# Logits ahead of x, and two even groups of 64 rows, in a top-2 mixture-of-experts dispatch kernel

## The chip, the cores and the metric

The kernel runs on one core of a Trainium2 chip. The metric is device time in microseconds of one execution; it is given as the median of several runs. The work on a core is shared between the engines VectorE (DVE in the profile), ScalarE (ACT), GpSimd (POOL), TensorE (PE, unused here) and SyncE (SP), and 16 DMA engines that move data between HBM, the large memory, and SBUF, the on-chip memory of 128 partitions. SP and ACT issue the DMA transfers here; each has a queue of its own (q1 and q10 in the profile).

## The reference

For each of 16 x 1024 = 16,384 tokens there is a vector x of 512 numbers and 8 router logits. The logits become probabilities, the two largest are scaled to sum to one, and the output has two copies of x for each token, one times each of the two weights, the smaller weight first:

```python
probs = np.exp(router_logits - logits_max)
probs = probs / np.sum(probs, axis=-1, keepdims=True)
topk_indices = np.argsort(probs, axis=-1)[..., -k:]
topk_probs = np.take_along_axis(probs, topk_indices, axis=-1)
topk_probs = topk_probs / np.sum(topk_probs, axis=-1, keepdims=True)
x_expanded = x[:, :, np.newaxis, :].repeat(k, axis=2)
return (x_expanded * topk_probs[..., np.newaxis]).astype(np.float32)
```

All is 32-bit floating point. The input x has 33.5 MB, the logits 0.5 MB, the output 67.1 MB.

## The kernel before, in words

The tokens are the rows of a matrix. They are cut into two groups (`GROUPS`, line 49), of 128 x 65 and 128 x 63 rows. Within a group partition p holds 65 (or 63) consecutive rows, so that what one partition reads or writes in HBM is one contiguous stretch: 65 rows of x are 130 KB, 65 rows of output 260 KB.

**Weights.** `top2_weights` (line 14) finds the largest and the second largest of the 8 logits of all 128 rows of each partition by a tournament of maxima and minima on VectorE (lines 27 to 37), subtracts them (line 40), and gets both weights as sigmoids of the difference on ScalarE (lines 42 and 43, into `WA`). The logits come in two transfers (lines 116 and 117), one for each group, which SP issues behind the first 16 rows of x.

**Products.** A group's x is loaded into `xs` in pieces of `LOADS` rows (line 51, issued at line 112). The multiplications at line 128 walk through the group by `plan`: each takes n rows from `xs`, doubles them, multiplies by the weights, and writes 2n rows. The output of the first 16 rows and of rows 32 to 47 goes into `osp`, a buffer of 16 doubled rows; that of the other rows goes back into `xs`, over rows which were already used. Where, is said by `over` (line 98): row r's output starts at `xs` row 2r - G, with G the rows of the group, so that the last output row ends at the end of `xs` (for rows 16 to 31 it is called with G = 32, and the output starts at `xs` row 0). `LAST` (line 54) lists the steps from row 48 on.

**Order.** Every product is followed by its store (line 136), which SP issues, but for the one of the first two rows, which ACT issues. Each engine executes its own instructions in the order in which they are written; SP therefore issues the loads of a group, then its stores one by one, each when its product is done, then the loads of the second group. A tile framework adds the waits that the use of buffers calls for: a load into rows of `xs` waits for the stores that still read them, a product into `osp` for the stores that read `osp`. Transfers issued by SP pass through the DMA engines in the order of issue, as the trace shows them.

Of the kernel before, what the change touches and what calls it, by code (L numbers as in the profile page):

```python
# [1 line left out]

# [4 lines left out]

F32 = mybir.dt.float32
ALU = mybir.AluOpType
ACTF = mybir.ActivationFunctionType  # L10
P = 128


def top2_weights(nc, pool, logits, M, E):

    hi, lo, n = None, None, E  # L20
    while n > 1:
        n //= 2
        if hi is None:
            a, b = logits[:, :, 0:n], logits[:, :, n : 2 * n]
            nhi = pool.tile([P, M, n], F32, tag=f"hi{n}")
            nlo = b
            nc.vector.tensor_tensor(nhi, a, b, op=ALU.max)  # L27
            nc.vector.tensor_tensor(nlo, a, b, op=ALU.min)  # L28
        else:
            a, b = hi[:, :, 0:n], hi[:, :, n : 2 * n]  # L30
            nhi = pool.tile([P, M, n], F32, tag=f"hi{n}")
            nlo = pool.tile([P, M, n], F32, tag=f"lo{n}")
            tmp = pool.tile([P, M, n], F32, tag=f"tmp{n}")
            nc.vector.tensor_tensor(tmp, lo[:, :, 0:n], lo[:, :, n : 2 * n], op=ALU.max)  # L34
            nc.vector.tensor_tensor(nlo, a, b, op=ALU.min)  # L35
            nc.vector.tensor_tensor(nlo, nlo, tmp, op=ALU.max)  # L36
            nc.vector.tensor_tensor(nhi, a, b, op=ALU.max)  # L37
        hi, lo = nhi, nlo
    dlt = pool.tile([P, M], F32, tag="dlt")
    nc.vector.tensor_tensor(dlt, hi[:, :, 0], lo[:, :, 0], op=ALU.subtract)  # L40
    WA = pool.tile([P, M, 2], F32, tag="WA")
    nc.scalar.activation(WA[:, :, 0], dlt, ACTF.Sigmoid, scale=-1.0)  # L42
    nc.scalar.activation(WA[:, :, 1], dlt, ACTF.Sigmoid, scale=1.0)  # L43
    return WA

GROUPS = [65, 63]

LOADS = [[2, 2, 4, 8, 17, 32], [16, 16, 31]]


LAST = [[(48, 9), (57, 8)], [(48, 15)]]


@with_exitstack
def kernel(
    ctx: ExitStack,
    tc: tile.TileContext,  # L60
    x: bass.AP,
    router_logits: bass.AP,
    k: bass.AP,
    out: bass.AP,
):
    nc = tc.nc
    B, S, D = x.shape
    E = router_logits.shape[-1]
    N = B * S
    assert int(k) == 2 and E == 8 and N == P * sum(GROUPS)  # L70
    M = N // P

    L = 16
    x_v, o_v, rl_v = [], [], []
    t0 = 0
    for n in GROUPS:
        t1 = t0 + P * n
        x_v.append(
            x.rearrange("b s d -> (b s) d")[t0:t1].rearrange("(p m) d -> p m d", p=P)
        )  # L80
        o_v.append(
            out.rearrange("b s k d -> (b s) k d")[t0:t1].rearrange(
                "(p m) k d -> p m k d", p=P
            )
        )
        rl_v.append(
            router_logits.rearrange("b s e -> (b s) e")[t0:t1].rearrange(
                "(p m) e -> p m e", p=P
            )
        )  # L90
        t0 = t1

    wpool = ctx.enter_context(tc.tile_pool(name="wpool", bufs=1))
    logits = wpool.tile([P, M, E], F32)
    xs = wpool.tile([P, max(GROUPS), D], F32)
    osp = wpool.tile([P, L, 2, D], F32)

    def over(r, n, G):

        a = 2 * r - G
        return xs[:, a : a + 2 * n, :].rearrange("p (r k) d -> p r k d", k=2)

    h = L // 2
    e = 2
    m0 = 0
    for g, G in enumerate(GROUPS):
        r = 0  # L110
        for n in LOADS[g]:
            nc.sync.dma_start(xs[:, r : r + n, :], x_v[g][:, r : r + n, :])  # L112
            r += n
            if g == 0 and r == L:

                nc.sync.dma_start(logits[:, :G], rl_v[0])  # L116
                nc.sync.dma_start(logits[:, G:], rl_v[1])
                WA = top2_weights(nc, wpool, logits, M, E)
        assert r == G
        begin = [(0, e, osp[:, :e]), (e, L - e, osp[:, e:])] if g == 0 else [(0, L, osp)]  # L120
        plan = begin + [
            (L, L, over(L, L, 2 * L)),
            (2 * L, h, osp[:, :h]),
            (2 * L + h, h, osp[:, h:]),
        ]
        plan += [(r, n, over(r, n, G)) for r, n in LAST[g]]
        for r, n, og in plan:
            nc.vector.tensor_tensor(  # L128
                og,
                xs[:, r : r + n, :].unsqueeze(2).to_broadcast([P, n, 2, D]),  # L130
                WA[:, m0 + r : m0 + r + n, :].unsqueeze(3).to_broadcast([P, n, 2, D]),
                op=ALU.mult,
            )

            queue = nc.scalar if n == e else nc.sync
            queue.dma_start(o_v[g][:, r : r + n], og)  # L136
        m0 += G


# [1 line left out]
_INS = ['x', 'router_logits', 'k']  # L141
_OUTS = [((16, 1024, 2, 512), 'float32')]

_NUMBERS = {'k': 2}


# [26 lines left out]
```

## Time and profile before

| what | value |
|---|---|
| median of 6 runs | 240.64 us (240.24 to 241.29) |
| profiled execution, its own time | 240.24 us |
| its span in the profile | 238.5 us |
| VectorE busy | 142.0 us (60%) in 23 instructions |
| ScalarE busy | 1.8 us |
| DMA | 101.19 MB in 3312 packets, mean 424 GB/s |
| multiplications (line 128) | 12, 138.2 us in all |
| longest wait of VectorE | 31.3 us, for a load of x |

The page cuts the span into 40 slices of about 6 us and gives for each the busy share of an engine in tenths; its DMA row is the mean over the 16 DMA engines. A queue's share is the time that its packets took, as a part of 16 engines' span. A packet is here what one partition gets or gives in one transfer, and each transfer ends with small packets that raise a semaphore. The trace also holds each packet's start, length and duration, which is where single packet times below come from. In the timeline a row has its start, its duration (of several merged instructions, from the first to the last), the engine ("SPq" is an issue by SP's queue), the line, the operation, what is written from what, and in brackets the idle time before it with what ended it.

### The profile page before, as it was taken

The page shows a single profiled execution, that of the slowest core. Times are in us where ns is not written, and L with a number is a line of the kernel's source. Part 1 is how long each engine was busy: PE and PEld are TensorE (multiplying, and loading weights), DVE is VectorE, ACT ScalarE, POOL GpSimd, SP SyncE. Part 2 cuts the span into 40 slices and gives each one's busy share as a digit, 9 for nine tenths or more (in the row PEclk, how much of TensorE's full clock was granted, in tenths as well). Part 3 has the DMA queues.
Part 4 walks back from the last instruction along what each step waited for, and adds up shares of the span by engine and source line. Part 5 has one row for each costly group of instructions (what it writes and reads, how often), then busy time and mean ns, then how long its engine had stood idle before and what let it go on. Part 6 is the DMA issues. An engine that isn't in the chain of part 4 may idle for free.

```text
span 238.5 us, 116 instructions
## 1 busy us (share of the span) xinstructions
DVE 142.0 (60%) x23; ACT 1.8 (1%) x3; POOL 0.2 (0%) x4
## 2 busy tenths in 40 slices
DVE  0058999990299699900000699999106999990000
ACT  2000000000000000000000000000000000000000
POOL 0000000000000000000000000000000000000000
DMA  7999999999798999999999999999998989999995
GB/s 254 441 464 402 539 407 396 374 462 462 341 517 352 440 440 440 440 402 478 440 434 412 423 484 437 415 473 396 396 484 374 506 352 440 440 440 429 495 423 237
DMA packets 3312, 101.19 MB, mean 424 GB/s; under 512 B 368, under 2 KB 496, under 8 KB 880
## 3 DMA queue, kind: packets, MB, share of 16 engines
q1 hardware_dynamic: 3168, 100.14, 97.8%
q10 hardware_dynamic: 144, 1.05, 1.0%
HBM read 34.08 MB, written 67.11 MB: 424 GB/s over the span
## 4 chain that ended last, share of the span: by engine, by line
DMA 43%; DVE 41%; issue 5%; SPq 1%; ACT 0%; DVEq 0%
DVE xs L128 22%; DVE osp L128 17%; DMA xs<-in_x_dram 13%; DMA out_dram<-osp 13%; DMA out_dram<-xs 12%; DMA logits<-in_router_logits_dram 5%; SPq L112 1%; DVE nhi L27 0%; SPq L116 0%; DVE logits L28 0%; DVE nlo L36 0%; DVE nhi L37 0%; DVE nlo L35 0%; DVE tmp L34 0%; SPq L136 0%
## 5 line engine op out<-in xcount | busy, mean ns | idle before, releaser
L128 DVE TENSOR_TENSOR osp<-xs,WA 128x8192 f32<-128x8192 f32 (+3 forms) x7 | 69.1, 9908 | 55.5 <-DMA xs<-in_x_dram 31.3
L128 DVE TENSOR_TENSOR xs<-xs,WA 128x16384 f32<-128x16384 f32 (+3 forms) x5 | 69.1, 13811 | 2.2 <-DMA out_dram<-xs 2.0
L27 DVE TENSOR_TENSOR nhi<-logits 128x512 f32<-128x512 f32 x1 | 0.7, 692 | 14.6 <-DMA logits<-in_router_logits_dram 14.6
L42 ACT ACT_TABLE_LOAD x1 | 1.3, 1283 | 0.7 <-PEq L154 0.7
L28 DVE TENSOR_TENSOR logits<-logits 128x512 f32<-128x512 f32 x1 | 0.7, 693 | 0.0
L35 DVE TENSOR_TENSOR nlo<-nhi 128x256 f32<-128x256 f32 (+1 forms) x2 | 0.7, 352 | 0.0
L37 DVE TENSOR_TENSOR nhi<-nhi 128x256 f32<-128x256 f32 (+1 forms) x2 | 0.7, 351 | 0.0
L36 DVE TENSOR_TENSOR nlo<-nlo,tmp 128x256 f32<-128x256 f32 (+1 forms) x2 | 0.7, 350 | 0.0
L42 ACT ACTIVATE WA<-dlt 128x128 f32<-128x128 f32 x1 | 0.3, 314 | 16.6 <-DVE dlt L40 16.6
L34 DVE TENSOR_TENSOR tmp<-logits 128x256 f32<-128x256 f32 x1 | 0.4, 417 | 0.0
L40 DVE TENSOR_TENSOR dlt<-nhi,nlo 128x128 f32<-128x128 f32 x1 | 0.3, 291 | 0.0
L43 ACT ACTIVATE WA<-dlt 128x128 f32<-128x128 f32 x1 | 0.3, 298 | 0.0
L34 DVE TENSOR_TENSOR tmp<-nlo 128x128 f32<-128x128 f32 x1 | 0.3, 283 | 0.0
L154 POOL MEMSET const-bfloat16-1.0<- 128x1 bf16 x1 | 0.1, 101 | 0.0
L154 POOL MEMSET const-uint8-127<- 128x1 uint8 x1 | 0.1, 101 | 0.0
L154 POOL MEMSET const-float32-0.0<- 128x1 f32 x1 | 0.1, 98 | 0.2 <-issue 0.2
L154 POOL MEMSET const-float32-1.0<- 128x1 f32 x1 | 0.1, 98 | 0.0
## 6 DMA issues: line engine op xcount, KB each, us to landing
out_dram<-osp SPq DMA_DIRECT2D x4, 4096.0 KB, 20.7
xs<-in_x_dram SPq DMA_DIRECT2D x2, 4096.0 KB, 29.9
xs<-in_x_dram SPq DMA_DIRECT2D x1, 7936.0 KB, 37.9
out_dram<-xs SPq DMA_DIRECT2D x1, 7680.0 KB, 23.2
out_dram<-osp SPq DMA_DIRECT2D x1, 7168.0 KB, 27.5
out_dram<-xs SPq DMA_DIRECT2D x1, 4608.0 KB, 20.4
xs<-in_x_dram SPq DMA_DIRECT2D x1, 4352.0 KB, 21.0
out_dram<-xs SPq DMA_DIRECT2D x1, 4096.0 KB, 21.6
```

Of the source, the lines that this page charges most:

```text
L27: nc.vector.tensor_tensor(nhi, a, b, op=ALU.max)
L28: nc.vector.tensor_tensor(nlo, a, b, op=ALU.min)
L34: nc.vector.tensor_tensor(tmp, lo[:, :, 0:n], lo[:, :, n : 2 * n], op=ALU.max)
L35: nc.vector.tensor_tensor(nlo, a, b, op=ALU.min)
L36: nc.vector.tensor_tensor(nlo, nlo, tmp, op=ALU.max)
L37: nc.vector.tensor_tensor(nhi, a, b, op=ALU.max)
L40: nc.vector.tensor_tensor(dlt, hi[:, :, 0], lo[:, :, 0], op=ALU.subtract)
L42: nc.scalar.activation(WA[:, :, 0], dlt, ACTF.Sigmoid, scale=-1.0)
L43: nc.scalar.activation(WA[:, :, 1], dlt, ACTF.Sigmoid, scale=1.0)
L112: nc.sync.dma_start(xs[:, r : r + n, :], x_v[g][:, r : r + n, :])
L128: nc.vector.tensor_tensor(og, xs[:, r : r + n, :].unsqueeze(2).to_broadcast([P, n, 2, D]), WA[:, m0 + r : m0 + r + n, :].unsqueeze(3).to_b ...
L154: nc = _bacc.Bacc("TRN2", target_bir_lowering=False, num_devices=1)
```

## The change

The groups become even, 64 rows per partition each, with loads, steps and last steps to match (17 becomes 16, 9 becomes 8, 31 becomes 32, 15 becomes 16). One partition's stretch is then 128 KB of x and 256 KB of output in either group. The logits come in one transfer instead of two: for each partition, two parts of 2 KB, one for each group. It is issued by SP ahead of the loads of x, and `top2_weights` is called right behind it.

```diff
-GROUPS = [65, 63]
-LOADS = [[2, 2, 4, 8, 17, 32], [16, 16, 31]]
-LAST = [[(48, 9), (57, 8)], [(48, 15)]]
+GROUPS = [64, 64]
+LOADS = [[2, 2, 4, 8, 16, 32], [16, 16, 32]]
+LAST = [[(48, 8), (56, 8)], [(48, 16)]]
...
-        rl_v.append(
-            router_logits.rearrange("b s e -> (b s) e")[t0:t1].rearrange(
-                "(p m) e -> p m e", p=P
-            )
-        )
         t0 = t1
+    rl_v = router_logits.rearrange("b s e -> (b s e)").rearrange(
+        "(g p r) -> p g r", g=len(GROUPS), p=P
+    )
 
     wpool = ctx.enter_context(tc.tile_pool(name="wpool", bufs=1))
     logits = wpool.tile([P, M, E], F32)
+    nc.sync.dma_start(
+        logits.rearrange("p m e -> p (m e)").rearrange(
+            "p (g r) -> p g r", g=len(GROUPS)
+        ),
+        rl_v,
+    )
+    WA = top2_weights(nc, wpool, logits, M, E)
+
     xs = wpool.tile([P, max(GROUPS), D], F32)
     osp = wpool.tile([P, L, 2, D], F32)
...
             nc.sync.dma_start(xs[:, r : r + n, :], x_v[g][:, r : r + n, :])
             r += n
-            if g == 0 and r == L:
-
-                nc.sync.dma_start(logits[:, :G], rl_v[0])
-                nc.sync.dma_start(logits[:, G:], rl_v[1])
-                WA = top2_weights(nc, wpool, logits, M, E)
         assert r == G
```

More of the change, by code (lines that the diff above doesn't have):

```diff
@@ L73 @@
     L = 16
-    x_v, o_v, rl_v = [], [], []
+    x_v, o_v = [], []
     t0 = 0
```

## The prediction

> **What bounds the kernel now.** I began with the slices of the page and its table of queues.
>
> ```profile
> DVE  0058999990299699900000699999106999990000
> ACT  2000000000000000000000000000000000000000
> POOL 0000000000000000000000000000000000000000
> DMA  7999999999798999999999999999998989999995
> ...
> q1 hardware_dynamic: 3168, 100.14, 97.8%
> q10 hardware_dynamic: 144, 1.05, 1.0%
> HBM read 34.08 MB, written 67.11 MB: 424 GB/s over the span
> ```
>
> VectorE has long idle stretches; the DMA engines have none. The packets of both queues took 97.8% + 1.0% = 98.8% of 16 engines' span, 235.6 us out of 238.5. The packet records of the trace agree: the first packet starts at 1.73 us, the last ends at 237.25, and in these 235.5 us all the places where an engine stood empty add up to 0.48 us (mean of the 16 engines). So the span is 1.7 us before the first packet, 235.5 us of packets back to back, and 1.2 us behind the last; the profiled run's own time, 240.24 us, has 1.74 us more around the span, and the median of the runs is another 0.40 us above it.
>
> Next I asked the timeline for what orders the queue.
>
> ```profile
> 0.72 1.80 SPq L112 DMA_DIRECT2D xs<-in_x_dram  x4
> 2.57 0.69 SPq L116 DMA_DIRECT2D logits<-in_router_logits_dram  x1
> 3.30 0.47 SPq L117 DMA_DIRECT2D logits<-in_router_logits_dram  x1
> 3.81 1.06 SPq L112 DMA_DIRECT2D xs<-in_x_dram  x2
> 14.64 0.69 DVE L27 TENSOR_TENSOR nhi<-logits 128x512 f32<-128x512 f32 x1 [14.64 <-DMA logits<-in_router_logits_dram]
> ...
> 36.44 0.35 SPq L136 DMA_DIRECT2D out_dram<-osp  x1
> ...
> 83.32 18.48 DVE L128 TENSOR_TENSOR xs<-xs,WA 128x9216 f32<-128x9216 f32 x2 [2.04 <-DMA out_dram<-xs]
> ...
> 102.25 21.60 SPq L112 DMA_DIRECT2D xs<-in_x_dram  x3
> ...
> 198.24 16.16 DVE L128 TENSOR_TENSOR xs<-xs,WA 128x15360 f32<-128x15360 f32 x1
> 214.43 0.33 SPq L136 DMA_DIRECT2D out_dram<-xs  x1
> ```
>
> VectorE starts late, at 14.64 us, and still each SP transfer is issued before the engines have drained those ahead of it. The store issued at 36.44 has its first packet at 46.23, behind the x loads; the last store, issued at 214.43, has its first packet at 218.57, so it waited 4.1 us in the ring. That backlog is what to check: an edit to an engine's order is worth nothing while it stays, and costs what it lacks if it goes.
>
> **The change, part by part.** *Bytes and packets.* 65 + 63 rows become 64 + 64, so the 101.19 MB stay. Packets of data stay at 128 for each x load and store and 256 for the logits (2,080 and 2,016 B before, 85 and 82 ns each; 2,048 B after, 83.5 ns by their mean). There is one transfer fewer, so one 9 ns semaphore packet less on each engine. Sum: -0.01 us. A packet of 32,768 B takes 1,213 ns and one of 65,536 B takes 2,418, a fixed 8 ns and 27.2 GB/s for each engine; 17-, 9-, 15- and 31-row transfers becoming 16, 8, 16 and 32 rows shift 8 ns at most. Zero.
>
> *The logits go to the head of SP.* L116 (0.69 us) and L117 (0.47 us) leave their place, and one issue comes in front of the x loads. How long an issue with two parts per partition takes isn't in the trace: between one x issue (0.38 us, after which the first packet came 0.63 us later) and L116 plus L117 (1.16 us), so the first packet comes 0 to 0.8 us later than now. I take the L116 row, 0.69 us in place of 0.38, less what earlier landing work hides: +0.2 us. The x issues follow every 0.43 us, while the logits hold each engine for 16 x 83.5 ns = 1.34 us, so no hole opens behind them. The slow first reads (the 4,096 B packets took 197 ns in the mean against 159 usual: 16 per engine, 0.61 us) are paid by whichever packets are first.
>
> The logits now land at about 4.5 us (1.9 + 1.34 + 0.6 for the slow first reads + 0.4 to signal), in place of 14.6. L27 to L40 take 3.9 us and the two sigmoids 0.55, so the first product starts at about 9 rather than 19.12. The second needs 16 rows of x, which land 1.2 us later than now (0.52 MB at 434 GB/s are ahead): 13.2 + 1.2 = 14.4, then 15.1 us of VectorE, its store issued at 29.6 instead of 36.44. Ahead of it in the ring are 18.35 MB (x, logits, ACT's store of the first two rows), 42.3 us, so its first packet goes at about 45.5, against 46.23. Seven microseconds earlier on VectorE lie wholly behind the loads. If that cover were gone the gain would be up to 7 us, but bytes forbid it.
>
> *Even groups.* With G=64 the outputs of rows 48 on start at xs row 32; with 65 they start at 31, inside the region that the store of rows 16 to 32 still reads. So VectorE's 2.04 us wait at 83.3 goes, and the second load of group two no longer waits for a store from xs. Behind SP's waiting load stood only the next loads. Both waits lie under a full ring. Is it still full later? Group two's first two loads (8.39 MB, 19.3 us) are queued when the last store of group one drains, which is what the third load waits for: covered. After the 16-row osp store lands, 16.78 MB (38.7 us) are put in the ring ahead of the last store, and VectorE needs 2 x 8.69 + 17.23 = 34.6 us, with issue and first packet 35.6. Its last step is now 16 rows (17.23 us by the row of that form, 16.16 for 15), so the cover shrinks from 4.1 to about 3 us but holds. Sum for both: 0.
>
> *The spacing of partitions in HBM.* Rows per partition set it: x 130 and 126 KB now, 128 KB after; output 260 and 252 KB now, 256 KB after. The row in the trace: 896 packets of 32,768 B, reads and writes alike, took 1,213 ns at the 10th, 50th and 90th percentile, so at today's spacing HBM slows nobody. The trace has no transfer at an exact power of two. The Trainium skill has a rule that speaks against the change: "DMA: Bandwidth & Descriptors", section "Latency and other measured facts", says that copies whose partitions lie a large power of two apart lose rate, 207 GB/s at 512 KiB, 164 at 2 MiB, 103 at 4 MiB, against 214 with a few KiB of padding. Its smallest case is twice our output's spacing and four times our input's. By the trace row alone this part costs 0. By the rule: time +3.4% at 512 KiB and +30% at 2 MiB, a factor of 9 over two doublings, 3 for each. My estimate from that page is then +1.1% for the stores and +0.4% for the loads: 67.11 MB at 434 GB/s are 154.7 us, so 1.75 us, and 33.55 MB are 77.4 us, so 0.3 us. Sum +2.05 us. Ends: 0, and 232 us at the 512 KiB figure, +7.9 us. No gain is possible here, since packets run at their full rate already. I take the estimate: the row nearest to the case is the page's, as the trace has none at a power of two and a saturated ring has nothing to hide a slower packet behind.
>
> Sum: -0.01 + 0.2 + 0 + 2.05 = +2.24 us. On the profiled 240.24 that is 242.5, and on the median 240.64 it is 242.9.
>
> **The rivals.** *The spacing doesn't matter and nothing else does.* The even packet times speak for it: the engines are the bound and HBM may have room left. Then the change doesn't do what it says, since earlier logits start a VectorE that wasn't awaited: 240.64 + 0.2 = 240.8, between 240.2 and 241.1.
>
> *Faster, by a stall that goes.* At about 43 us the last 16 packets of the group's x load took 3.06 us in the mean instead of 2.42, 0.64 us on every engine at once. ACT's store of two rows (landing 25.7 us after its issue at 21.44) is still sharing the engines there. After the change it is issued at about 11.5 and has left the engines before that place. If the meeting of three streams made the stall, it goes, and the issue at the head may cost nothing: 240.64 - 0.64 = 240.0. It decides if at least 0.5 us of it disappear. Against it: a weaker stall (0.14 us) stands at the end of the second group's load at about 158 us, where ACT's queue is empty.
>
> *A hole before the last store.* If VectorE were 3 us later at the end than worked out, the ring would run dry before the last store, and each further microsecond would be lost: 1 to 3 us, so 241.6 to 243.6. The 3 us cover speaks against it, and slower packets would widen it.
>
> **How the numbers follow.** A difference under 0.2%, 0.48 us, is about what a measurement of this kernel can't tell from none. Spacing slows the packets: 0.52. Nothing matters: 0.26. The stall goes: 0.18. A hole: 0.04. Slower is 0.52 + 0.04 = 0.56, since the spacing's case begins where it passes 0.2%. The likeliest case gives 242.9, its own range 241.3 to 248.5. The range for all reaches from 240.0, the faster case's centre (some 0.09 lie below), to 247.5, near the upper end of the spacing's cost with the start's (0.09 above).
>
> **What would show it.** Earlier logits: L27 at 4 to 6 us, the first product at about 9, and SP's first store near 29.6 rather than 36.4. No order gain: that store lands about where it does now, 64 us. Full ring: DMA slices at 9 throughout and queue shares summing to 98 to 99%. Spacing: packets of 32,768 B spread above 1,213 ns and GB/s under 430 in the middle of the span, more in the stores; all steady at 1,213 would refute it. The hole would stand as an empty slice near 215 us. Wrong in the other direction would be a first packet much after 2 us, or a span that grows while packet times don't.

## The result, and the profile after

The changed kernel took 240.7 us (median of 31 runs, 240.37 to 241.13) beside 240.35 us of the kernel before (70 runs, 240.08 to 241.29): the ratio is 1.0014, with a 95% interval of 1.0009 to 1.0018. That is 0.35 us, under the 0.2% named in the prediction, and the rival "nothing matters" had given 240.8. The forecast change, 2.24 us, was six times too large.

On four of the five chips used for the experiments the times of the kernel before lie in two heaps, 240.2 to 241.3 and 241.5 to 242.8 us, so that a ratio from there mixes the two, and "lower runs" below means those under 241.5 us.

First the parts of the changed kernel's page that answer to those shown of before:

```profile
DVE  1859999800399999400000999997008999990000
ACT  2000000000000000000000000000000000000000
POOL 0000000000000000000000000000000000000000
DMA  7999998999989899999999998989999998999894
...
q1 hardware_dynamic: 3152, 100.14, 97.8%
q10 hardware_dynamic: 144, 1.05, 1.0%
q14 instruction: 1, 0.00, 0.0%
HBM read 34.08 MB, written 67.11 MB: 424 GB/s over the span
```

VectorE's busy digits have moved to the left by more than a slice at the start. The DMA row, the queues' shares and the 424 GB/s are those of before. Then the timeline (start, duration, engine and line; in brackets the wait and what ended it):

```profile
0.73 0.44 SPq L92 DMA_DIRECT2D logits<-in_router_logits_dram  x1
1.22 2.98 SPq L117 DMA_DIRECT2D xs<-in_x_dram  x6
4.77 0.69 DVE L27 TENSOR_TENSOR nhi<-logits 128x512 f32<-128x512 f32 x1 [4.77 <-DMA logits<-in_router_logits_dram]
...
9.24 2.29 DVE L128 TENSOR_TENSOR osp<-xs,WA 128x2048 f32<-128x2048 f32 x1 [0.58 <-ACT WA L43]
...
14.79 15.09 DVE L128 TENSOR_TENSOR osp<-xs,WA 128x14336 f32<-128x14336 f32 x1 [3.26 <-DMA xs<-in_x_dram]
29.91 0.35 SPq L136 DMA_DIRECT2D out_dram<-osp  x1
...
63.45 17.29 DVE L128 TENSOR_TENSOR osp<-xs,WA 128x8192 f32<-128x8192 f32 x2 [16.31 <-DMA out_dram<-osp]
...
80.78 17.42 DVE L128 TENSOR_TENSOR xs<-xs,WA 128x8192 f32<-128x8192 f32 x2
...
214.64 0.33 SPq L136 DMA_DIRECT2D out_dram<-xs  x1
```

In the kernel before, the row that answers to the one at 63.45 us was

```profile
63.99 17.29 DVE L128 TENSOR_TENSOR osp<-xs,WA 128x8192 f32<-128x8192 f32 x2 [10.32 <-DMA out_dram<-osp]
```

The logits land ten microseconds earlier, the first product starts at 9.24 us, SP's first store is issued at 29.91 instead of 36.44, and it lands at 63.4 us, where before it landed at 64. The 2.04 us wait of VectorE at 83 us is gone, but the wait for `osp` ahead of it has grown from 10.3 to 16.3 us, and a wait of 3.3 us for x has come in front. All that was saved on VectorE is waited away behind the full ring, the queue of transfers that are issued and not yet moved.

Where are the 0.35 us? From the packet records one can add up, for each packet that took over 30 ns more than 8 ns plus its bytes at 27.2 GB/s, what it took too long, and divide by 16 engines. In the two profiles: the first packet starts at 1.83 us instead of 1.73 (+0.10); slow packets cost 1.68 us instead of 1.44 (+0.24: at the head 0.77 for 0.61, at the turn from loads to stores near 43 us 0.49 for 0.64, at the two turns of group two, near 118 and 157 us, 0.40 for 0.17); empty places 0.49 for 0.48. That makes +0.35, and the last packet ends at 237.61 instead of 237.25, +0.36. The span is 238.9 us for 238.5, and the profiled run's own time 240.67 for 240.24. All these are single executions, so the split of some tenths is rough: a second profile of the changed kernel had 0.61 at the head and 0.21 at the two turns, a third 0.02 and 0.21, and in the third the engines stood empty longer instead (its packets took 235.13 us for each engine, for 236.02 in the first). What all three have against three of the kernel before is a first packet at 1.80 to 1.83 us for 1.73 to 1.74, and a last packet that ends at 237.46 to 237.61 us for 237.23 to 237.42.

### The profile page after: what moved, and what is told of

It is laid out like the page before. It is cut to its first block, busy times and chain, and to the rows that moved or that the text cites. A ratio compares the mean times of both kernels' runs of the same rounds, so it can differ in the third digit from the quotient of the medians.

```text
span 238.9 us, 113 instructions
## 1 busy us (share of the span) xinstructions
DVE 142.1 (59%) x23; ACT 1.8 (1%) x3; POOL 0.2 (0%) x4
## 4 chain that ended last, share of the span: by engine, by line
DMA 46%; DVE 39%; issue 4%; SPq 1%; DVEq 0%
DMA out_dram<-osp 27%; DVE osp L128 24%; DMA xs<-in_x_dram 19%; DVE xs L128 14%; SPq L117 1%; SPq L92 0%; SPq L136 0%; DVEq L128 0%
## 5 line engine op out<-in xcount | busy, mean ns | idle before, releaser
L128 DVE TENSOR_TENSOR xs<-xs,WA 128x16384 f32<-128x16384 f32 (+1 forms) x5 | 69.1, 13811 | 0.2
L27 DVE TENSOR_TENSOR nhi<-logits 128x512 f32<-128x512 f32 x1 | 0.7, 694 | 4.8 <-DMA logits<-in_router_logits_dram 4.8
```

Of the source, the lines that this page charges most:

```text
L128: nc.vector.tensor_tensor(og, xs[:, r : r + n, :].unsqueeze(2).to_broadcast([P, n, 2, D]), WA[:, m0 + r : m0 + r + n, :].unsqueeze(3).to_b ...
```

## The experiments

### Which half of the change carries it

Each half alone, twice: the logits first with the old groups,

```diff
     logits = wpool.tile([P, M, E], F32)
+    nc.sync.dma_start(logits[:, : GROUPS[0]], rl_v[0])
+    nc.sync.dma_start(logits[:, GROUPS[0] :], rl_v[1])
+    WA = top2_weights(nc, wpool, logits, M, E)
...
-            if g == 0 and r == L:
-
-                nc.sync.dma_start(logits[:, :G], rl_v[0])
-                nc.sync.dma_start(logits[:, G:], rl_v[1])
-                WA = top2_weights(nc, wpool, logits, M, E)
```

> Groups stay at 65 and 63 rows; only the logits move ahead of x, as two transfers of 2,080 and 2,016 B per partition. Theory A (the changed kernel's +0.34 us is all start: a later first packet and more slow first reads): +0.3 to +0.4 us over the kernel before, first packet about 0.1 us later, slow first reads cost about 0.8 us per engine instead of 0.6. Theory B (the difference is the even groups: the longer last store and the ends of the packets' streams): 0.0 us. Either way L27 starts at about 5 us instead of 14.6 and gains nothing.

> Groups of 65 and 63, logits ahead of x. The first try gave 241.0 in its lower runs against 240.6, with other runs of both kernels 2 us higher. Theory A (start): +0.3 us or more, since the two logits transfers cost two issues ahead of x. Theory B (even groups): 0.0 us. If both halves cost, +0.15 to +0.3.

and the even groups with the logits where they were:

```diff
-GROUPS = [65, 63]
+GROUPS = [64, 64]
-LOADS = [[2, 2, 4, 8, 17, 32], [16, 16, 31]]
+LOADS = [[2, 2, 4, 8, 16, 32], [16, 16, 32]]
-LAST = [[(48, 9), (57, 8)], [(48, 15)]]
+LAST = [[(48, 8), (56, 8)], [(48, 16)]]
```

> Groups of 64 and 64 rows only; the logits stay behind the first 16 rows of x, as two transfers of 2 KB per partition. Theory A (start): 0.0 us against the kernel before. Theory B (even groups): +0.3 to +0.4 us. The recorded theory of spacing in HBM said +2 us; after the changed kernel's trace, with 32,768 B packets at 1,213 ns, I expect none of it, and packets of the same duration here.

> Groups of 64 and 64, logits behind 16 rows of x. The first try gave 240.8 in its lower runs against 240.6. Theory A (start): 0.0 us. Theory B (even groups): +0.3 us. If both halves cost, +0.1 to +0.2, with the cost in the slow packets at the turn from stores to loads at 118 us, at the turn from loads to stores at 156 us and in the uneven end of the 16 engines.

> The changed kernel itself, beside the next two, so that the halves are compared with the whole on one chip. +0.3 us against the kernel before (ratio 1.0014, as first measured).

On the first chip the logits first took 241.50 us (22 runs, 11 of them above 241.5), the even groups 240.93 (7 of 22 above), the kernel before 240.71 (25 of 75 above); ratios 1.0022 (1.0002 to 1.0041) and 0.9998 (0.9972 to 1.0024). On the second chip the logits first took 242.04 us (11 of 12 above 241.5), the even groups 241.38 (5 of 12), the whole change 240.52 (none of 12; 240.35 to 240.69), the kernel before 240.80 with 16 of 35 above and 240.37 in its lower runs. The lower runs of the even groups lay 0.2 us above those of the kernel before on the first chip and 0.8 on the second.

Neither theory holds as it was put. The halves don't add up to the whole: on the second chip, against the lower runs of the kernel before, the logits first cost 1.67 us alone and 0.15 us together with the even groups. What makes the even groups alone slower in their lower runs is not shown. For the logits first the profile shows where the time goes. In the table of stretches (busy times by engine, then granted TensorE clock, the DMA share and GB/s; a packet counts where it starts, so a short stretch may exceed 1), the changed kernel's first profile has

```profile
2.00:6.00 4.00, 1.19 (x2) 0.01 (x1) 0.00 (x0) 1.00 1.02 344
...
236.00:240.00 4.00, 0.00 (x0) 0.00 (x0) 0.00 (x0) 1.00 0.00 0
```

and the second run of the logits first with the old groups

```profile
2.00:6.00 4.00, 1.84 (x4) 0.01 (x1) 0.00 (x0) 1.00 0.86 238
...
236.00:240.00 4.00, 0.00 (x0) 0.00 (x0) 0.00 (x0) 1.00 0.25 108
```

Between 2 and 6 us the engines move 238 GB/s in place of 344, and at the end data packets still start after 236 us. Of the 60 packets of 4,096 B that start between 3 and 5 us in its records 37 take the usual 159 ns, but seven take 1.2 to 1.7 us, so that the mean is 394; in the changed kernel every one takes 159. Single engines stand empty for about 1.5 us there (the records don't name the engine of a packet, so this follows from which packet begins where another ends). Not all engines lose the same, and what one loses at the head it still lacks at the end: the last packets of the 16 engines end 2.25 us apart, for 0.56 in the kernel before and 0.77 in the changed one. That the engines don't take over work from each other is plainest in the run with old groups, logits first and one big first load, further below: there two engines begin their last packet of 2.27 us at 237.5 us, when the other 14 have ended. Between 50 and 112 us nothing is slow in either profile.

What differs at the head is the form of the logits' transfer: one of two parts in the change, two transfers in this half, since groups of 65 and 63 rows have parts of unequal length. The section "The form of the head" below tests it.

### Is the spacing of partitions felt at all?

Partitions twice as far apart, first in everything, then in x or the output alone:

```diff
-        x_v.append(
-            x.rearrange("b s d -> (b s) d")[t0:t1].rearrange("(p m) d -> p m d", p=P)
-        )
+        x_v.append(
+            x.rearrange("b s d -> (b s) d").rearrange("(p m) d -> p m d", p=P)[
+                :, t0 // P : t1 // P
+            ]
+        )
```

(the same for `o_v` where the output is meant, and for the logits in the first of the three). With x or the output alone, products go to other rows of the output than the reference has them; these two kernels show the traffic, not the values.

> The changed kernel with each partition's 128 rows in one stretch: partitions lie 256 KiB apart in x and 512 KiB in the output, in both groups, and the logits come as one 4 KB part. The page's rule at its own smallest case, 207 against 214, would give +3.4% on the stores (155 us), +5 us, and my tripling would give +0.9 us for the loads: 246 us, with 32,768 B and 65,536 B packets above 1,213 and 2,418 ns. Theory that spacing doesn't matter within these sizes for transfers between HBM and SBUF: 240.4 to 240.7, the same packet times, and perhaps 0.1 us less than the changed kernel for the larger logits packets.

> The changed kernel with x alone at 256 KiB between partitions in both groups; the output stays at 256 KiB and the logits at two 2 KB parts. The rows of x go to other output rows than the reference has them: the traffic is measured, not the values. With both doubled, the slow packets were x loads, 13 to 16 us and 118 to 126 us, 1.7 us per engine in all, no store among them. Theory that the spacing of reads makes it: +1.2 to +1.6 us against the changed kernel, with slow 32,768 B loads at the same places. Theory that the output's 512 KiB makes it, by disturbing the loads that follow: 0.0 us against the changed kernel.

> The changed kernel with the output alone at 512 KiB between partitions; x stays at 128 KiB and the logits at one transfer of two parts. The products go to other output rows than the reference has them: the traffic is measured, not the values. With x alone doubled the time was 240.8 (0.3 us above the changed kernel beside it); with both doubled 242.3. If the output's spacing makes the difference, 242 us, with slow loads of 32,768 B right behind group one's stores (118 to 126 us). The page's figure for 512 KiB, +3.4% on all stores, would be +5 us, 245.5. If it took both spacings together: 240.5 to 240.9.

Measured: 242.34 us for both (22 runs, 241.81 at the lowest; lower runs of the kernel before 240.62), 240.83 for x alone (240.52 for the changed kernel beside it), 242.00 for the output alone (241.80 to 242.43; lower runs of before 240.56). So 512 KiB between the output's partitions cost 1.4 us, both together 1.7, and x at 256 KiB 0.3. The stretches up to group two's first turn and behind it, of the changed kernel's first profile:

```profile
16.00:116.00 100.00, 65.79 (x6) 0.00 (x0) 0.00 (x0) 1.00 1.01 433
116.00:126.00 10.00, 0.00 (x0) 0.00 (x0) 0.00 (x0) 1.00 1.02 436
126.00:155.00 29.00, 23.50 (x2) 0.00 (x0) 0.00 (x0) 1.00 1.04 451
```

and of the output at 512 KiB:

```profile
16.00:116.00 100.00, 65.47 (x6) 0.00 (x0) 0.00 (x0) 1.00 1.01 433
116.00:126.00 10.00, 0.00 (x0) 0.00 (x0) 0.00 (x0) 1.00 0.97 380
...
161.00:236.00 75.00, 40.07 (x4) 0.00 (x0) 0.00 (x0) 1.00 1.00 433
236.00:240.00 4.00, 0.00 (x0) 0.00 (x0) 0.00 (x0) 1.00 0.61 262
```

For 100 us of loads and stores the wide output runs at 433 GB/s, as the changed kernel does. Behind these it loses where one direction ends and the other begins: 16 loads right behind group one's stores near 119 us took 1,875 ns in the mean instead of 1,213, and the last 16 of the group near 157 us 3,600 instead of 2,418. Slow packets at these two turns cost 2.05 us per engine with the output at 512 KiB, 0.40, 0.21 and 0.21 us in three profiles of the changed kernel (256 KiB), and 0.17, 0.12 and 0.09 us in three of the kernel before (260 and 252 KiB). The last step, from 0.13 to 0.27 in the mean, is small against the scatter; the first is not. Over all profiles with these spacings and engines in step, seven of even groups have 0.16 to 0.40 us and four of old groups 0.09 to 0.17, so some of that step is likely real, but the sizes of the transfers change with the spacing there. No kernel had its partitions this far apart without a power of two, say with some KiB of padding, so whether the power of two makes the loss at the turns, or the distance alone, is not shown. The expectation that the reads' own spacing makes it fell: the slow packets are reads, but x at 256 KiB alone left 0.39 there.

The Trainium skill's figure ("DMA: Bandwidth & Descriptors", section "Latency and other measured facts") leads to an estimate of +5 us at 512 KiB, 207 for 214 GB/s all through the stores. Here the measurement decides: about 1.5 us, at the turns.

The two profiles of the kernel before come from these runs, which were to show its upper heap:

> The kernel before, unchanged, for a second profile. On two chips a third to a half of its runs took about 242.3 us, the rest 240.4, while the changed kernel's runs all lay between 240.3 and 241.1. If this profile falls among the higher ones, the theory of the head (small loads of x, 4 KB packets, read slowly and with empty engines between 3 and 6 us, as in the run of uneven groups with logits first) expects 1.5 to 2 us more of slow packets and empty places before 16 us, engines that end 1 to 2 us apart, and everything between as before. The rival, that the loss lies at the turns between loads and stores (43, 118, 158 us), expects slow packets there and a common end.

> The kernel before once more, for a profile; as for the first of these two. At a half to a third of its runs near 242.3 us, one of the two should show it.

They took 240.41 and 240.25 us, so both fell in the lower heap, on a chip where all 16 runs of it did. What the kernel before does in its upper runs was not caught.

### The form of the head

Even groups, both halves of the logits first, in two transfers; in two transfers on two queues; and only the first half ahead of x. The diffs against the changed kernel, cut to the issue:

```diff
-    nc.sync.dma_start(
-        logits.rearrange("p m e -> p (m e)").rearrange(
-            "p (g r) -> p g r", g=len(GROUPS)
-        ),
-        rl_v,
-    )
+    nc.sync.dma_start(logits[:, : GROUPS[0]], rl_v[0])
+    nc.sync.dma_start(logits[:, GROUPS[0] :], rl_v[1])
```

with `nc.scalar` in the second line for two queues; with the second line and `top2_weights` behind the first 16 rows of x for one half.

> The changed kernel, but with the logits ahead of x in two transfers of 2 KB per partition (one for each group) in place of one of two parts. If the two transfers make the slow head of the run with uneven groups: 241.5 to 242.3 us, with 4,096 B packets at 200 to 400 ns. If the even groups keep the head fast: 240.5 to 240.8 us as in the changed kernel, with 4,096 B packets at 159 ns.

> Groups of 64 and 64, both halves of the logits ahead of x in two transfers, the second on ACT's queue instead of SP's. If the trouble is that SP's x loads come one issue later or that two short transfers follow each other in one ring: 240.5 to 240.8. If two transfers of 2 KB parts disturb the x loads behind them however they are issued: 241.5 to 242.3.

> Groups of 64 and 64; only group one's logits ahead of x, 2 KB per partition in one transfer; group two's behind the first 16 rows of x. If a second small transfer at the head is the trouble: 240.4 to 240.8 us, 4,096 B packets at 159 ns from 4 us on. If any transfer of single 2 KB parts at the head starts it: 241.5 to 242.3, with empty engines between 3 and 6 us.

Two transfers on SP: 242.00 us (241.14 to 242.68, lower runs of before 240.31), with even groups. Two queues: 240.49 (12 runs, 240.42 to 241.41). One half first: 242.13, 8 of 12 above 241.5. So neither the groups nor the count of two makes the slow head. The form doesn't decide a single run, but how many are slow: with one or two transfers of one 2 KB part per partition at the front of SP's queue, and the loads of x behind them, 11 of 22, 11 of 12, 5 of 6 and 8 of 12 runs were above 241.5 us, and of the kernel before beside them 25 of 75, 16 of 35, none of 16 and 13 of 35. One transfer of two such parts kept the head steady (none of the 55 runs of the changed kernel was above), and so did the second half on ACT's queue (none of 12), and, by its one profile, one 4 KB part (in the run with both spacings doubled, 0.58 us of slow packets at the head). Ends of the 16 engines: 1.71 us apart with two transfers, 2.75 with one half, 1.30 on two queues (in a profile that is its slowest run, 241.41), 0.68 to 0.85 in three profiles of the changed kernel.

Last, the loads behind the logits: one load of 16 rows in place of 2, 2, 4 and 8 rows, in three kernels: in the kernel before (with one product and one store for the first 16 rows, so no transfer on ACT), in old groups with logits first, and in the changed kernel.

```diff
-LOADS = [[2, 2, 4, 8, 16, 32], [16, 16, 32]]
+LOADS = [[16, 16, 32], [16, 16, 32]]
```

(this is the third's; in the old groups the first list is 16, 17, 32).

> The kernel before, with the first 16 rows in one load in place of four (2, 2, 4, 8), and one product and one store of 16 rows in place of 2 and 14, so no transfer on ACT. If the start's cost is one of packets (8 ns each and the slow first reads being paid per packet): 24 data packets and 3 semaphore packets fewer per engine at the head, 8 and 1 fewer for the store: -0.3 us, plus up to 0.4 us of slow first reads: 239.7 to 240.1. If slow first reads last a fixed time whatever the packets' size: -0.3 us, no more. If ACT's store were part of the 0.64 us stall at 43 us, that goes too. VectorE's later start (about 2 us later stores) costs nothing while the ring is full.

> Groups of 65 and 63 with logits first, as in the run that took 242.0, but the first 16 rows of x in one load in place of 2, 2, 4 and 8. If the small first loads make the slow head: 240.3 to 240.8 us and runs close together. If not the size of the first loads but their places in HBM: 241.5 to 242.3 us still, with the first 32,768 B packets slow.

> The changed kernel with the first 16 rows of x in one load in place of 2, 2, 4 and 8. Uneven groups with two logits transfers and this big load took 242.9. If the two transfers at the head are what sets engines apart: 240.3 to 240.6 here, 24 data and 3 semaphore packets per engine fewer (0.22 us), runs close together. If the large first load is at fault: above 241.5.

In the kernel before: 240.98 us (one of 22 runs above 241.5, 25 of 75 of before). It lacks the upper heap, but lies 0.36 above before's lower runs: the 0.29 us of packets were saved (the sum of all packets at full rate fell from 234.19 to 233.90 us), and lost again at the turn near 42 us (1.01 us of slow packets for 0.64) and in engines that end 1.25 us apart. In old groups with the logits first: 242.88 (8 of 11 above), and two engines end at 239.7 and 239.8 us where the other 14 end by 237.0. So the small loads of x are not what it takes. In the changed kernel: 240.46 (240.25 to 240.68), ratio 0.9977 (0.9957 to 0.9998) to the kernel before, whose runs were 13 of 35 in the upper heap there, and 240.56 in the lower.

To see whether that beats both, it ran once more beside the changed kernel:

> The changed kernel beside its version with one big first load, on one chip. +0.15 to +0.35 us against the lower runs of the kernel before, runs close together.

> The changed kernel with the first 16 rows of x in one load. 24 data packets (8 ns each) and 3 semaphore packets (9 ns) fewer per engine are 0.22 us: 0.1 to 0.3 us under the changed kernel beside it, equal to the lower runs of the kernel before or a little under them, and without its runs near 242. If the saved packets are lost again in slow reads behind the head (0.45 us between 18 and 22 us in the first profile): equal to the changed kernel.

240.53 us for the changed kernel (240.41 to 240.79) and 240.48 for the one with the big load (240.33 to 240.89), the kernel before 241.56, with 12 of 23 runs in the upper heap and 240.39 in the lower; ratios 0.9964 (0.9939 to 0.9988) and 0.9961 (0.9935 to 0.9987). The two can't be told apart. The 0.22 us of packets saved come back as slow reads between 12 and 40 us (0.44 us for 0.04), which was the second of the two things expected. Both are steadier than the kernel before, and where its runs are split, faster in the mean; against its lower runs neither is.

## Why the prediction was wrong

**The step that failed is the spacing of partitions, +2.05 us, at the choice between row and page.** The trace's row said 1,213 ns for every 32,768 B packet, the page's rule led to +1.1% on the stores, and the rule was taken because the row had no power of two in it. In the changed kernel these packets took 1,213, 1,213 and 1,218 ns at the 10th, 50th and 90th percentile. What was refuted is the form of the cost, a rate for every byte. Something of the kind exists, at turns between directions: 2.05 us of slow packets with the output at 512 KiB, some 0.15 at 256 above the kernel before. With 0.15 in the place of 2.05 us the prediction's sum is 0.34, beside 0.35 measured; as the 0.15 rests on single executions, so close an agreement is luck. Extrapolating a loss of rate from the page's copies of 16 KiB for each partition, between HBM tensors, to transfers of up to 64 KB between HBM and SBUF had no support in this trace, and the test of the rule at its own smallest case shows it about three times too dear here (+1.5 us, for 5).

**The logits at the head, +0.2 us: right in size.** The issue took 0.44 us (forecast 0.69, bounds 0.38 and 1.16), the first packet came 0.10 us later, and slow first reads cost 0.16 us more in one profile and nothing more in another; in the third empty places stood for them. L27 at 4.77 us (4.5, though the terms given for it add up to 4.24; in a second profile it was 4.29), the first product at 9.24 (9), the second at 14.79 (14.4), its store issued at 29.91 (29.6), all as worked out, and all worth nothing. That the transfer's form could matter was seen only as a range of issue times; the experiments found 1.5 us and more in it, by another way: engines that get out of step at the head. The change has the steady form, so its own forecast wasn't hurt; that was luck, as nothing in the prediction told this form from the others.

**The waits that go, 0: right.** Both went, and VectorE's time moved to the wait for `osp`.

**The cover before the last store, 3 us: right.** Issued at 214.64, first packet at 217.52: 2.9 us. There is no hole.

**The rival of the vanishing stall: wrong in its cause.** ACT's store left the engines at 28.5 us, before the stall, and the stall stayed: 0.49, 0.58 and 0.48 us in three profiles, 0.64, 0.74 and 0.59 in the kernel before. It does vanish where the engines were set apart at the head (0 to 0.09 us in five such profiles), but then they end apart.

**The chances.** The case that came had 0.26, the failed one 0.52. The rival "nothing matters" had the right mechanism and, at 240.8, nearly the number. The upper side of the range was built from the same extrapolation as the failed term.

## What to carry to other kernels

When packets of every size run at one fixed rate and the ring never empties, as here, what is left to gain or lose is the head, the turns between loads and stores, and how far apart the 16 engines end; reordering engines is worth nothing until the backlog is gone. A rule about rates should be put beside the packet durations of the trace before it is scaled to a size that nobody measured. And since the engines took nothing over from each other here, look at when each engine ends, not only at their mean: a delay of some engines in the first 6 us is still there at the end.

## What had not been expected

- Engines that get out of step at the head don't come together again: with one or two transfers of one 2 KB part per partition at the front of SP's queue the 16 ends lay 1.71 to 3.42 us apart in four profiles, of runs of 241.6 to 243.0 us, and 0.99 in a fifth, of 241.0 us; in the other fifteen it was 0.51 to 1.30. Why this form does it, and two parts, a 4 KB part or a second queue mostly don't, stays open. The slow ones begin with 0.26 MB on the engines, the steady ones with 0.52 (in one transfer or on two queues), but no run sets the size of the first transfer against its form, and the kernel before begins with 0.52 MB of x and isn't steady. In three of the four, SP's own issues of x also took longer (six in 3.83 and 4.48 us, for 2.87 to 2.98 in the changed kernel; the last two in 2.25, for 1.06 in the kernel before), in the fourth they did not; cause or effect isn't shown. Open, too, is whether the upper heap of the kernel before, which starts with 4 KB loads of x, is the same thing, as none of its profiles fell there.
- All engines in step stall together when a group's loads give way to stores, near 43 us: 0.5 to 1.0 us on each, in every kernel whose engines were in step but the changed one with the big first load (0.18 and 0.25).
- Outside the first 40 us and the turns near 43, 118 and 157 us, slow packets cost 0.01 us or less in all twenty profiles: neither the spacing nor VectorE's work beside them is seen to touch a running stream.
